# One search in lockstep on two engines, a buffer of its own for the pooling input, and two key blocks in one bank, in a hybrid attention layer

## The chip, the cores and the metric

One Trainium2 chip, one of its cores. The metric is the device time of one execution in microseconds (us), the median of several runs; lower is better. Engines are named as in the profile: PE (matrix multiply; PEld its weight loads), DVE (vector), ACT (scalar, activations), POOL (GpSimd), SP (issues the DMAs).

## What is computed

A layer of 1024 tokens and 1024 channels in float32. One input projection of the normalized tokens feeds three mixers, whose gated outputs are concatenated, projected and added to the input:

```python
h = rmsnorm(x, norm_g[layer])
z = jnp.einsum('bld,dc->blc', h, w_in[layer])
(pv, pg, dq, dk, dv, dg, iq, ik, iw, fq, fk, fv, fg, ff) = split_columns(z)
a_out = pool_mixer(pv, pool_w[layer], pool_scale[layer]) * jax.nn.silu(pg)
...
b_out = b_o.reshape(B, L, DSA_WIDTH) * jax.nn.silu(dg)
...
c_out = c_o.reshape(B, L, FOX_WIDTH) * jax.nn.silu(fg)
mixed = jnp.concatenate([a_out, b_out, c_out], axis=-1)
x = x + jnp.einsum('blc,cd->bld', mixed, w_out[layer])
```

The pooling mixer takes trailing-window means (windows 2, 4, 8, 16). The sparse mixer has an indexer (8 heads of 32 channels) that scores each key for each query as a weighted sum of relu'd dots; a query attends, in 6 heads, to its 256 best keys. The forgetting mixer is causal attention in 6 heads with a cumulative bias.

## The kernel before

Tokens are tiled by 128 (tiles 0 to 7). Every product of float32 data is split: a value is rounded to a high part (ACT copies it), the rest is a low part (DVE or POOL subtracts), and a projection sums three matmuls, high by high, high by low and low by high (`mm3`, L457). A chunk of a projection is 24 such matmuls of 384 or 512 columns into one PSUM bank of three (`pj`); then ACT and DVE evacuate it: L718 and L719 (queries and keys), L732 and L734 (gates), L659 and L660 (values), L1042 (pooling input, on ACT alone). The next matmul into that bank waits for the evacuation. Weights are split on ACT (L689, L433) and POOL (L690, L434).

The indexer's scores of tiles 2 to 7 (tile i has 128(i+1) keys) are summed on DVE (L602) and POOL closes each with a small fill (L605). Then `search` finds, for each query, the 256th best score by bisection over the 31 bits of a float: a round counts the scores above a trial value in each tile, compares the counts with 256 and sets the next bit. One search counts tiles 6 and 7 on ACT (L768, a sign with an accumulated sum, read out by a second instruction), another counts tiles 2 to 5 on DVE (L772). Each has its own three small DVE steps a round: L786, L788 and L789; L788 needs the counts of all tiles of its search, and the next round's counts need L789. There are 32 counts of each tile. `finish` turns the thresholds into masks (L813 to L843), with a correction (`fix`) for tiles counted on ACT.

The pooling mixer works in two halves, m = 0 and 1. A half has an input buffer `v`, filled by two L1042 on ACT, and two work buffers; POOL adds shifted copies (L1049), DVE takes the means (L1065 to L1069) and PE maps them (L1073). The three buffers of one half come from one tag, `pq`, that has three slots, so the second half's `v` gets a slot when the first half is through with it.

Attention goes in units of two heads by 512 queries: scores (L918, L921), maximum (L929), exponentials (L940), then for each block of 128 keys transpositions on PE (L950), their split by ACT (L957) and DVE (L959), and the products with the values (L963, L965). The last two key blocks of a head have only 256 and 128 columns. A unit ends with L975 to L998; at the end the output projection (`outproj`) runs on all engines.

Nothing of the order is written by hand. `Plan.schedule` is a list scheduler: from estimated durations (`t_mm`, `t_act`, `t_dve`, `t_pool`), priorities and free buffer slots it fixes one order for each engine before the run, and each engine runs its own in that order. A changed estimate, tag or list of tiles so moves instructions all over the kernel.

## Time and profile before

| what | value |
|---|---|
| median of 3 runs | 678.64 us (677.1 to 679.01) |
| the profiled execution | 675.91 us |
| its span | 674.1 us |
| PE busy | 631.3 us, 94% of the span |
| DVE busy | 524.4 us, 78% |
| ACT busy | 395.9 us, 59% |
| POOL busy | 202.5 us, 30% |

The span runs from the first to the last instruction of the program; the execution's own time is 1.8 us longer. The page shows the busy time of each engine, the same in 40 slices of the span with the clock granted to PE, and the costliest groups of instructions. The trace behind it answers questions on one engine, line or stretch: a timeline (instructions in order, equal neighbours merged, in brackets the idle time before and what ended it), waits, groups by line, and sums over a stretch. L457 is line 457 of the kernel before.

### The profile page before, as it was taken

To read this page: it belongs to the slowest core of one execution; us is meant where nothing else is said; L and a number is where in the kernel's file an instruction comes from. 1 tells how busy PE (TensorE), PEld (TensorE's weight loads), DVE (VectorE), ACT (ScalarE), POOL (GpSimd) and SP (SyncE) were. 2 spreads that over 40 slices of the span, in tenths; PEclk is the share of its full clock that TensorE was granted. 3 is DMA by queue.
4 is the path that set the end of the run, shared out by engine and by line. 5 is a ranking of instruction groups with operands and counts; after the bars stand their busy time and mean duration, and the time that the engine had idled before them with its cause. 6 is when DMAs were issued, how large, how long until landed. Compare 5 with 4: busy or idle time off the path is not lost. (4 is left out here: it accounts for less than half of the span.)

```text
span 674.1 us, 10707 instructions
## 1 busy us (share of the span) xinstructions
PE 631.3 (94%) x3278; PEld 529.4 (79%) x3278; DVE 524.4 (78%) x1363; ACT 395.9 (59%) x904; POOL 202.5 (30%) x218
## 2 busy tenths in 40 slices
PE   7899999999999399879999899999899999989995
PEld 5798777799888399667878688888778777778884
DVE  5978999999999989989997666758576868655322
ACT  5745777566666545531658467778567869731211
POOL 3610324520036512114442442512031435132311
PEclk9999999999999699989999999999899999999999
DMA  7707554640035323744647668569874555266211
GB/s 227 222 1 199 152 167 110 184 132 3 16 97 138 84 104 106 220 144 135 209 156 236 188 171 236 180 189 276 227 233 151 184 175 172 64 196 202 103 63 62
DMA packets 98439, 103.02 MB, mean 153 GB/s; under 512 B 10983, under 2 KB 67399, under 8 KB 98382
## 3 DMA queue, kind: packets, MB, share of 16 engines
q1 hardware_dynamic: 98382, 102.34, 50.8%
q8 instruction: 26, 0.43, 0.3%
q14 instruction: 31, 0.25, 0.1%
HBM read 72.35 MB, written 29.96 MB: 152 GB/s over the span
## 5 line engine op out<-in xcount | busy, mean ns | idle before, releaser
L457 PE MATMUL bank<-RA 128*128 128x512 f32 (+2 forms) x2016 | 492.0, 381 | 16.5 <-ACT FA L1042 10.5
L457 PEld LDWEIGHTS bank<-RA 128*128 128x128 f32 x2016 | 361.2, 190 | 67.6 <-ACT FA L1042 10.9
L957 ACT ACTIVATE RA<-bank 128x512 fp32r<-128x512 f32 (+3 forms) x144 | 67.8, 488 | 62.9 <-PE bank L950 58.8
L772 DVE TENSOR_SCALAR_CACHE_REDUCE FA<-FA 128x384 bf16<-128x384 f32 (+3 forms) x128 | 103.4, 808 | 1.6
L690 POOL TENSOR_TENSOR RA<-FA,RA 128x512 fp32r<-128x512 f32 x44 | 63.8, 1461 | 126.8 <-ACT RA L689 122.0
L768 ACT ACTIVATE FA<-FA 128x896 bf16<-128x896 f32 x64 | 69.8, 1090 | 52.6 <-DVE FA L789 42.9
L929 DVE CUSTOM_DVE_ANT_0 FA<-bank,FA 128x512 f32<-128x512 f32 (+3 forms) x144 | 77.4, 552 | 28.5 <-PE bank L921 9.9
L959 DVE TENSOR_TENSOR RA<-bank,RA 128x512 fp32r<-128x512 f32 (+3 forms) x144 | 77.0, 553 | 23.1 <-ACT RA L957 14.0
L940 ACT ACTIVATE FA<-FA 128x512 f32<-128x512 f32 (+3 forms) x144 | 86.8, 607 | 7.3 <-DVE FA L935 7.2
L950 PE MATMUL bank<-FA 128*128 128x128 f32 x432 | 79.4, 276 | 3.2 <-DVE RA L959 2.2
L950 PEld LDWEIGHTS bank<-FA 128*128 128x128 f32 x432 | 55.7, 141 | 21.3 <-DVE RA L959 5.3
L918 PE MATMUL bank<-RA 128*128 128x512 f32 (+3 forms) x144 | 52.3, 365 | 6.0 <-DVE FA L929 2.9
L602 DVE SCALAR_TENSOR_TENSOR FA<-FA 128x512 f32<-128x512 f32 (+3 forms) x70 | 54.2, 798 | 1.9
L921 PE MATMUL bank<-RA 128*128 128x512 f32 (+3 forms) x144 | 51.1, 361 | 2.6 <-DMA RA<-qk_dq 2.4
L965 PE MATMUL bank<-RA 128*128 128x512 f32 (+3 forms) x144 | 53.4, 375 | 0.0
L963 PE MATMUL bank<-RA 128*128 128x512 f32 (+3 forms) x144 | 49.2, 342 | 0.5 <-ACT RA L957 0.5
L594 ACT ACTIVATE FA<-bank 128x512 f32<-128x512 f32 (+3 forms) x80 | 39.7, 527 | 16.3 <-DVE FA L602 6.8
L925 POOL TENSOR_TENSOR FA<-FA 128x128 f32<-128x128 f32 x48 | 25.6, 541 | 71.2 <-DMA FA<-nf_d 34.9
L918 PEld LDWEIGHTS bank<-RA 128*128 128x128 f32 x144 | 27.1, 189 | 13.3 <-DVE FA L929 7.7
L921 PEld LDWEIGHTS bank<-RA 128*128 128x128 f32 x144 | 27.3, 191 | 6.2 <-DMA RA<-qk_dq 2.6
L963 PEld LDWEIGHTS bank<-RA 128*128 128x128 f32 x144 | 27.3, 190 | 6.3 <-ACT RA L957 2.1
L997 POOL TENSOR_TENSOR FA<-FA 128x512 f32<-128x512 f32 x12 | 16.2, 1347 | 52.9 <-DVE FA L993 27.6
(145 smaller groups left out, 688.1 us busy)
## 6 DMA issues: line engine op xcount, KB each, us to landing
FA<-in_w_in_dram SPq DMA_DIRECT2D x60, 256.0 KB, 3.4
FA<-in_x_dram SPq DMA_DIRECT2D x15, 512.0 KB, 3.6
RA<-qk_fq SPq DMA_DIRECT2D x48, 128.0 KB, 3.9
RA<-qk_dq SPq DMA_DIRECT2D x48, 128.0 KB, 2.8
RA<-qk_dk SPq DMA_DIRECT2D x36, 128.0 KB, 3.3
FA<-in_w_out_dram SPq DMA_DIRECT2D x16, 256.0 KB, 2.8
out_dram<-FA SPq DMA_DIRECT2D x7, 512.0 KB
RA<-qi SPq DMA_DIRECT2D x24, 128.0 KB, 3.0
```

The costliest lines, as they stand in the source:

```text
L457: M(lambda: nc.tensor.matmul(p()[:, :n], fa(), fb(), start=st, stop=sp), n, keys, [p], pr)
L690: G(lambda raw=raw, s=s: nc.gpsimd.tensor_tensor(Wl()[:, s, :], raw(), f32(Wh()[:, s, :]), op=OP.subtract), 512, [raw, (Wh, kh)], [(Wl, kh ...
L768: A(lambda c=c, i=i, jk=jk, s=s: nc.scalar.activation(jk(), SC[i](), AF.Sign, bias=s(), scale=-1.0, accum_out=cn()[:, c:c + 1]), n, sck(i) ...
L772: V(lambda c=c, i=i, jk=jk, s=s: nc.vector.tensor_scalar(jk(), SC[i](), s(), None, op0=OP.is_lt, op1=OP.add, accum_out=cn()[:, c:c + 1]), ...
L918: M(lambda s=s, k=k, n=n, j=j, hd=hd: nc.tensor.matmul(s()[:, :n], qx()[:, hd, j * 128:j * 128 + 128], k()[:, hd, :n], start=True, stop=Fa ...
L921: M(lambda s=s, k=k, n=n, j=j, hd=hd: nc.tensor.matmul(s()[:, :n], ql()[:, hd, j * 128:j * 128 + 128], k()[:, hd, :n], start=False, stop=T ...
L929: V(lambda s=s, Pt=Pt, n=n, u=u, j=j, mx=mx, bias=bias: nc.vector.tensor_tensor_reduce(Pt()[:, :n], s()[:, :n], bias()[:, u * 512:u * 512 ...
L940: A(lambda Pt=Ps[j][u], n=n, j=j, u=u, hd=hd, nm=nm: nc.scalar.activation(Pt()[:, :n], Pt()[:, :n], AF.Exp, bias=nm()[:, j:j + 1], accum_o ...
L950: M(lambda pt=pt, j=j, Pt=Ps[j][kb // 4], c=kb % 4 * 128: nc.tensor.transpose(pt()[:, j * 128:j * 128 + 128], Pt()[:, c:c + 128], ident()) ...
L957: A(lambda ph=ph, pt=pt, c=c: nc.scalar.activation(ph()[:, c], pt()[:, c], AF.Copy), n, [pt], [ph], pr, psum=True)
L959: V(lambda ph=ph, pl=pl, pt=pt, c=c: nc.vector.tensor_tensor(pl()[:, c], pt()[:, c], f32(ph()[:, c]), op=OP.subtract), n, [pt, ph], [pl], pr)
L963: M(lambda o=o, v=v, ph=ph, c=c, kb=kb: nc.tensor.matmul(o()[:, c], v(), ph()[:, c], start=(kb == 0), stop=False), n, kv + [ph], [o], pr)
```

## The change

1. `search` is called once, for all six tiles: tiles 5, 6 and 7 are counted on ACT, tiles 2, 3 and 4 on DVE, in lockstep: one L788 needs the counts of all six. `finish` goes over all tiles in order and corrects tiles 5, 6 and 7.
2. The pooling's `v` has a tag of its own, `pv`, with two slots, one of them new memory; `pq` keeps two slots for the work buffers.
3. The last two key blocks of a head are transposed into one bank and split by one ACT and one DVE instruction of 384 columns.
4. The scheduler takes a transposition for 0.07 us instead of 0.107, and adds 0.085 us to a PE instruction that follows one and is none itself.

```diff
-                    t = free[e]
+                    t = free[e] + (0.085 if e == PE and was_tr and not o.tr else 0.0)
...
+            if e == PE:
+                was_tr = o.tr
...
-    return max(n * 0.41667e-3 + 0.003, 0.107)
+    return 0.07 if n < 0 else max(n * 0.41667e-3 + 0.003, 0.107)
...
-    lay("F", f1 + 9 * KB, [("pq", 4160, 3), ("pw", KB, 1)], 1)
+    lay("F", f1 + 9 * KB + 4160, [("pq", 4160, 2), ("pw", KB, 1)], 1)
...
-    FSZ, RSZ = max(f2, f3), r3
+    FSZ, RSZ = max(f2, f3) + 4160, r3
+    P.tag("pv", "F", 4160, [FSZ - 4160, f1 + 9 * KB], 1)
...
-    M = lambda fn, n, r, w, pr=0.0: P.op(PE, fn, t_mm(n), r, w, pr)
+    M = lambda fn, n, r, w, pr=0.0: P.op(PE, fn, t_mm(n), r, w, pr, tr=n < 0)
...
-    def search(tiles, a):
-        nq = len(tiles)
-        eng = ACT if a == "a" else DVE
+    def search(tiles, on_act):
+        nq, a = len(tiles), "s"
         t0, _ = carve(nq)
         t1, _ = carve(nq)
         cn, _ = carve(nq)
@@ -754,21 +758,22 @@
         k = lambda nm, c=None: (cc, "s" + a, nm, c)
         for c, i in enumerate(tiles):
             n = (i + 1) * 128
-            G(lambda c=c, n=n: nc.gpsimd.memset(th()[:, c:c + 1],
-                                                float(n - 2 * TOPK if eng == ACT else n - TOPK) + 0.5), 1, [],
+            G(lambda c=c, i=i, n=n: nc.gpsimd.memset(th()[:, c:c + 1],
+                                                     float(n - (2 * TOPK if i in on_act else TOPK)) + 0.5), 1, [],
               [k("th")], 0)
         pr = PR_SEL
 
         def count(t, kt):
-            for c, i in enumerate(tiles):
+            for c, i in sorted(enumerate(tiles), key=lambda x: x[1] not in on_act):
                 n = (i + 1) * 128
                 s = (lambda: 0.0) if t is None else (lambda c=c: t()[:, c:c + 1])
-                jk = P.new("jka" if eng == ACT else "jkv", [128, n], BF)
-                if eng == ACT:
+                if i in on_act:
+                    jk = P.new("jka", [128, n], BF)
                     A(lambda c=c, i=i, jk=jk, s=s: nc.scalar.activation(jk(), SC[i](), AF.Sign, bias=s(), scale=-1.0,
                                                                          accum_out=cn()[:, c:c + 1]), n,
                       sck(i) + kt, [jk, k("cn", c)], pr, acc=True)
...
-    def finish(tiles, t, kt, cn, a, fix):
+    def finish(tiles, on_act, t, kt, cn, a):
         pr = PR_SEL
         v = nc.vector
-        if fix:
-            nz, knz = carve(len(tiles))
-            V(lambda: v.tensor_scalar(nz().bitcast(I32), t().bitcast(I32), 0x7fffffff, None, op0=OP.bitwise_and), 2,
-              [kt], [knz], pr)
-            V(lambda: v.tensor_scalar(nz(), nz(), 2.0 ** -126, None, op0=OP.is_ge), 2, [knz], [knz], pr)
-            V(lambda: v.tensor_tensor(t(), t(), nz(), op=OP.mult), 2, [kt, knz], [kt], pr)
-        for c, i in enumerate(tiles):
+        na = len(on_act)
+        nz, knz = carve(na)
+        ta = lambda: t()[:, :na]
+        V(lambda: v.tensor_scalar(nz().bitcast(I32), ta().bitcast(I32), 0x7fffffff, None, op0=OP.bitwise_and), na,
+          [kt], [knz], pr)
+        V(lambda: v.tensor_scalar(nz(), nz(), 2.0 ** -126, None, op0=OP.is_ge), na, [knz], [knz], pr)
+        V(lambda: v.tensor_tensor(ta(), ta(), nz(), op=OP.mult), na, [kt, knz], [kt], pr)
+        for c, i in sorted(enumerate(tiles), key=lambda x: x[1]):
+            fix = i in on_act
...
-            for kb in range(nkb):
-                j0 = max(0, kb - 4 * g)
+            v = lambda kb, h=h: VV[kb]()[:, h * 128:h * 128 + 128]
+            for kbs in [(kb,) for kb in range(nkb - 2)] + [(nkb - 2, nkb - 1)]:
                 pt = P.new("pt", [128, 512])
-                for j in range(j0, 4):
-                    M(lambda pt=pt, j=j, Pt=Ps[j][kb // 4], c=kb % 4 * 128: nc.tensor.transpose(
-                        pt()[:, j * 128:j * 128 + 128], Pt()[:, c:c + 128], ident()), 128,
-                      [Ps[j][kb // 4], k_ident], [pt], pr)
+                cols = []
+                for kb in kbs:
+                    j0 = max(0, kb - 4 * g)
+                    d = 256 if kb == nkb - 1 else 0
+                    cols.append((kb, j0, slice(j0 * 128 - d, 512 - d)))
+                    for j in range(j0, 4):
+                        M(lambda pt=pt, j=j, d=d, Pt=Ps[j][kb // 4], c=kb % 4 * 128: nc.tensor.transpose(
+                            pt()[:, j * 128 - d:j * 128 - d + 128], Pt()[:, c:c + 128], ident()), -128,
+                          [Ps[j][kb // 4], k_ident], [pt], pr)
                 ph = P.new("ph", [128, 512], F32R)
                 pl = P.new("pl", [128, 512], F32R)
-                c = slice(j0 * 128, 512)
-                n = 512 - j0 * 128
+                c = slice(min(x.start for _, _, x in cols), 512)
+                n = 512 - c.start
                 A(lambda ph=ph, pt=pt, c=c: nc.scalar.activation(ph()[:, c], pt()[:, c], AF.Copy), n, [pt], [ph],
                   pr, psum=True)
                 V(lambda ph=ph, pl=pl, pt=pt, c=c: nc.vector.tensor_tensor(pl()[:, c], pt()[:, c], f32(ph()[:, c]),
                                                                            op=OP.subtract), n, [pt, ph], [pl], pr)
-                v = lambda kb=kb, h=h: VV[kb]()[:, h * 128:h * 128 + 128]
-                kv = [(VV[kb], "h"), (VV[kb], "l")]
-                M(lambda o=o, v=v, ph=ph, c=c, kb=kb: nc.tensor.matmul(o()[:, c], v(), ph()[:, c], start=(kb == 0),
-                                                                       stop=False), n, kv + [ph], [o], pr)
-                M(lambda o=o, v=v, pl=pl, c=c, kb=kb, nkb=nkb: nc.tensor.matmul(
-                    o()[:, c], v(), pl()[:, c], start=False, stop=(kb == nkb - 1)), n, kv + [pl], [o], pr)
+                for kb, j0, c in cols:
+                    kv = [(VV[kb], "h"), (VV[kb], "l")]
+                    M(lambda o=o, v=v, ph=ph, c=c, j0=j0, kb=kb: nc.tensor.matmul(
+                        o()[:, j0 * 128:], v(kb), ph()[:, c], start=(kb == 0), stop=False), 512 - j0 * 128, kv + [ph], [o],
+                      pr)
+                for kb, j0, c in cols:
+                    kv = [(VV[kb], "h"), (VV[kb], "l")]
+                    M(lambda o=o, v=v, pl=pl, c=c, j0=j0, kb=kb, nkb=nkb: nc.tensor.matmul(
+                        o()[:, j0 * 128:], v(kb), pl()[:, c], start=False, stop=(kb == nkb - 1)), 512 - j0 * 128,
+                      kv + [pl], [o], pr)
...
-        v, s1, s2 = (P.new("pq", [128, W]) for _ in range(3))
+        v, s1, s2 = P.new("pv", [128, W]), P.new("pq", [128, W]), P.new("pq", [128, W])
...
-    sa = search([6, 7], "a")
-    sv = search([2, 3, 4, 5], "v")
-    finish([2, 3, 4, 5], *sv, False)
-    finish([6, 7], *sa, True)
+    on_act = [5, 6, 7]
+    tiles = on_act + [2, 3, 4]
+    finish(tiles, on_act, *search(tiles, on_act))
```

In the other places (`op`, `norm`, `idx_k`, `idx_tile`, `forget`, `unit`) a transposition only gets the width -128, by which the scheduler knows it.

What this does to the order of the instructions is shown at three places. In the rows of the changed kernel line numbers are its own: L768 became L772, L772 became L777, L786, L788 and L789 became L791, L793 and L794, L689 L694, L732 L737, L659 and L660 L664 and L665, and L1042 L1058.

ACT at the pooling, before; the counts of the search are L768, the weight splits L689:

```order
L768 ACTIVATE FA<-FA 128x896
L768 ACTIVATE FA<-FA 128x1024
L689 ACTIVATE RA<-FA 128x512 x2
L1042 ACTIVATE FA<-bank_66 128x512
L1042 ACTIVATE FA<-bank_65 128x512
L659 ACTIVATE RA<-bank_71 128x3x2x64
```

The same place now:

```order
L1058 ACTIVATE FA<-bank_71 128x512
L772 ACTIVATE FA<-FA 128x1024
L772 ACTIVATE FA<-FA 128x768
L772 ACTIVATE FA<-FA 128x896
L772 ACTIVATE FA<-FA 128x1024
L1058 ACTIVATE FA<-bank_65 128x512
L694 ACTIVATE RA<-FA 128x512 x2
L772 ACTIVATE FA<-FA 128x768
L772 ACTIVATE FA<-FA 128x896
L664 ACTIVATE RA<-bank_66 128x3x2x64
```

The second half's two evacuations stood together, after the splits; now they stand a round and a third apart, each as its chunk comes.

DVE in one round of the search, in the stretch of the sparse values, before (128x2 belongs to the search on ACT, 128x4 to the one on DVE):

```order
L786 TENSOR_SCALAR FA<-FA 128x2
L772 TENSOR_SCALAR FA<-FA 128x384
L786 TENSOR_SCALAR FA<-FA 128x4
L772 TENSOR_SCALAR FA<-FA 128x512
L772 TENSOR_SCALAR FA<-FA 128x640
L660 TENSOR_TENSOR RA<-bank_66,RA 128x3x128
L788 TENSOR_TENSOR FA<-FA 128x2
L772 TENSOR_SCALAR FA<-FA 128x768
L789 SCALAR_TENSOR_TENSOR FA<-FA 128x2
L788 TENSOR_TENSOR FA<-FA 128x4
L786 TENSOR_SCALAR FA<-FA 128x2
L789 SCALAR_TENSOR_TENSOR FA<-FA 128x4
```

A round there now:

```order
L777 TENSOR_SCALAR FA<-FA 128x384
L791 TENSOR_SCALAR FA<-FA 128x6
L777 TENSOR_SCALAR FA<-FA 128x512
L777 TENSOR_SCALAR FA<-FA 128x640
L665 TENSOR_TENSOR RA<-bank_71,RA 128x3x128
L793 TENSOR_TENSOR FA<-FA 128x6
L794 SCALAR_TENSOR_TENSOR FA<-FA 128x6
```

The count of 768 is gone from DVE, and one trio of small steps is left, with the evacuation of a value chunk just ahead of it.

ACT at the end of the search, before, up to the first gate of the forgetting mixer:

```order
L768 ACTIVATE FA<-FA 128x1024
L689 ACTIVATE RA<-FA 128x512 x2
L768 ACTIVATE FA<-FA 128x896
L768 ACTIVATE FA<-FA 128x1024
L768 ACTIVATE FA<-FA 128x896
L732 ACTIVATE FA<-bank_65 128x512
```

And now:

```order
L772 ACTIVATE FA<-FA 128x1024
L694 ACTIVATE RA<-FA 128x512 x2
L772 ACTIVATE FA<-FA 128x768
L772 ACTIVATE FA<-FA 128x896
L772 ACTIVATE FA<-FA 128x1024
L772 ACTIVATE FA<-FA 128x768
L772 ACTIVATE FA<-FA 128x896
L772 ACTIVATE FA<-FA 128x1024
L737 ACTIVATE FA<-bank_65 128x512
```

The first gate stood before the last count; now it stands behind the last round, the fifth after the last value chunk.

## Rows read from the trace of the kernel before

**Rows 1.** Page, part 1: busy us (share of the span) x instructions of each engine.

```profile
PE 631.3 (94%) x3278; PEld 529.4 (79%) x3278; DVE 524.4 (78%) x1363; ACT 395.9 (59%) x904; POOL 202.5 (30%) x218
```

**Rows 2.** Timeline of PE, 195 to 305 us; in brackets the idle time before and its releaser.

```profile
194.79 27.47 PE L457 MATMUL bank<-RA 128*128 128x512 f32 x126
232.81 15.71 PE L457 MATMUL bank<-RA 128*128 128x384 f32 x75 [10.55 <-ACT FA L1042]
...
292.24 12.98 PE L457 MATMUL bank<-RA 128*128 128x512 f32 x49 [3.75 <-DVE FA L734]
```

**Rows 3.** PE's waits, whole span: us in total, times, longest us.

```profile
PE bank L918 <- DVE FA L929: 2.9, 3, 2.2
PE bank L921 <- DMA RA<-qk_dq: 2.4, 1, 2.4
...
PE bank L918 <- DMA RA<-qk_fq: 2.0, 1, 2.0
```

**Rows 4.** Three stretches: busy us by engine, granted clock (PEclk), DMA share, GB/s.

```profile
75.00:136.00 61.00, 59.17 (x257) 46.17 (x258) 59.67 (x100) 42.23 (x88) 20.66 (x18) 1.00 0.54 149
224.50:238.00 13.50, 5.19 (x16) 5.19 (x17) 13.36 (x45) 8.28 (x15) 5.41 (x6) 0.50 0.25 73
292.80:296.00 3.20, 3.20 (x9) 2.44 (x8) 3.20 (x8) 1.14 (x2) 0.00 (x0) 0.50 0.42 164
```

**Rows 5.** Timeline of ACT: first count of tile 7, the late evacuation, the first gate.

```profile
136.05 1.06 ACT L768 ACTIVATE FA<-FA 128x1024 bf16<-128x1024 f32 x1 [3.54 <-POOL FA L605]
...
232.16 1.09 ACT L1042 ACTIVATE FA<-bank 128x512 f32<-128x512 f32 x2 [3.29 <-DVE FA L789]
...
290.86 0.60 ACT L732 ACTIVATE FA<-bank 128x512 f32<-128x512 f32 x1 [3.17 <-DMA mx_p<-FA]
```

**Rows 6.** DVE by line: counts, then compare and step: busy us, mean ns.

```profile
L772 DVE TENSOR_SCALAR_CACHE_REDUCE FA<-FA 128x384 bf16<-128x384 f32 (+3 forms) x128 | 103.4, 808 | 1.6
...
L788 DVE TENSOR_TENSOR FA<-FA 128x4 int32<-128x4 f32 (+1 forms) x62 | 16.3, 278 | 1.0 <-ACT FA L768 1.0
L789 DVE SCALAR_TENSOR_TENSOR FA<-FA 128x4 int32<-128x4 int32 (+1 forms) x62 | 15.1, 260 | 0.1
```

**Rows 7.** Timeline of ACT in one round: tile 6, its readout, tile 7, its readout.

```profile
202.18 1.04 ACT L768 ACTIVATE FA<-FA 128x896 bf16<-128x896 f32 x1 [0.29 <-DVE FA L789]
203.13 0.19 ACT L768 ACTIVATION_READ_ACCUMULATOR FA<-FA 128x1 f32 x1
203.35 1.15 ACT L768 ACTIVATE FA<-FA 128x1024 bf16<-128x1024 f32 x1
204.41 0.19 ACT L768 ACTIVATION_READ_ACCUMULATOR FA<-FA 128x1 f32 x1
```

**Rows 8.** Timeline of all engines at 242.38 us: DVE's step, then ACT's next count.

```profile
242.38 0.16 DVE L789 SCALAR_TENSOR_TENSOR FA<-FA 128x2 int32<-128x2 int32 x1
...
242.63 1.04 ACT L768 ACTIVATE FA<-FA 128x896 bf16<-128x896 f32 x1 [1.29 <-DVE FA L789]
```

**Rows 9.** ACT by line and shape: value evacuation and weight split.

```profile
L659 ACT ACTIVATE RA<-bank 128x384 fp32r<-128x384 f32 x16 | 7.6, 477 | 4.8 <-PE bank L457 4.7
...
L689 ACT ACTIVATE RA<-FA 128x512 fp32r<-128x512 f32 x44 | 27.1, 630 | 7.1 <-DMA FA<-nf_d 1.9 <-DMA FA<-in_w_in_dram 1.9 <-PE bank L457 1.8
```

**Rows 10.** Timeline of PE in attention: a lone transposition, and three in a run.

```profile
394.78 0.27 PE L950 MATMUL bank<-FA 128*128 128x128 f32 x1
...
402.24 0.49 PE L950 MATMUL bank<-FA 128*128 128x128 f32 x3
402.48 0.48 PE L965 MATMUL bank<-RA 128*128 128x512 f32 x1
402.80 0.39 PE L963 MATMUL bank<-RA 128*128 128x512 f32 x1
```

**Rows 11.** ACT by line and shape: the last two evacuations of a head.

```profile
L957 ACT ACTIVATE RA<-bank 128x256 fp32r<-128x256 f32 x24 | 9.1, 380 | 17.5 <-PE bank L950 17.4
...
L957 ACT ACTIVATE RA<-bank 128x128 fp32r<-128x128 f32 x24 | 6.6, 273 | 5.5 <-PE bank L950 5.5
```

More of the change, by code (lines that the diff above doesn't have):

```diff
@@ L77 @@
 class Op:
-    __slots__ = ("eng", "fn", "dur", "pr", "seq", "deps", "bufs", "outs", "end", "left", "bytes", "lag")
+    __slots__ = ("eng", "fn", "dur", "pr", "seq", "deps", "bufs", "outs", "end", "left", "bytes", "lag", "tr")
 class Plan:
@@ L516, in norm @@
                 c = (4 * u + k) * 128
-                M(lambda p=p, k=k, c=c: nc.tensor.transpose(p()[:, k, :], xt()[:, c:c + 128], ident()), 128,
+                M(lambda p=p, k=k, c=c: nc.tensor.transpose(p()[:, k, :], xt()[:, c:c + 128], ident()), -128,
                   [(xt, u), k_ident], [p], pr)
@@ L557, in idx_k @@
         pk = P.new("s", [128, 512])
[L558 removed]
+        M(lambda: nc.tensor.transpose(pk()[:, :128], zt()[:, 0, :], ident()), -128, [zt, k_ident], [pk], pr)
         kk = lambda: KI()[:, i * 128:i * 128 + 128]
@@ L569, in idx_tile @@
         for u in range(2):
-            M(lambda u=u: nc.tensor.transpose(pq()[:, u, :], Z[i]()[:, u * 128:u * 128 + 128], ident()), 128,
+            M(lambda u=u: nc.tensor.transpose(pq()[:, u, :], Z[i]()[:, u * 128:u * 128 + 128], ident()), -128,
               [Z[i], k_ident], [pq], pr)
@@ L771, in count @@
                 else:
+                    jk = P.new("jkv", [128, n], BF)
                     V(lambda c=c, i=i, jk=jk, s=s: nc.vector.tensor_scalar(jk(), SC[i](), s(), None, op0=OP.is_lt,
@@ L974, in unit @@
         pr8 = P.new("pt", [128, 512])
-        M(lambda: nc.tensor.transpose(pr8()[:8, :128], rc().rearrange("p h j -> p (h j)"), ident()), 128,
+        M(lambda: nc.tensor.transpose(pr8()[:8, :128], rc().rearrange("p h j -> p (h j)"), ident()), -128,
           [rc, k_ident], [pr8], pr)
```

7 lines of the change are left out of this document (4 added, 3 removed).

## The prediction, made before the changed kernel ran

> **What bounds the kernel now.** I read the page first: PE is busy 94% of the span [rows 1], so a gain is either less work on PE or less waiting by PE. The counts of PE's instructions do not change, so it must be waiting. The timeline of PE shows where: the two longest waits of the run, 10.55 us for L1042 (pooling input) and 3.75 us for L734 (a gate) [rows 2], and 2.0 us for a query load close to them [rows 3]. The sums over stretches show what waiting costs on top: after the first wait PE's granted clock is 0.50 (1.2 of 2.4 GHz) and PE works 5.19 us in that stretch, half of it lost, 2.6 us; after the second it works 3.20 us at 0.50, 1.6 us lost [rows 4]. Together 10.55 + 3.75 + 2.0 + 2.6 + 1.6 = 20.5 us.
>
> Both long waits come from the search. The timeline of ACT [rows 5] shows L1042 starting at 232.16, after 3.29 us of idle ACT: its buffer was held by the pooling's first half, whose DVE steps stood in DVE's queue between the counts. The first gate of the forgetting mixer starts at 290.86, behind the last rounds of the search. So from 136.05, when tile 7 is first counted, to 290.86 the two searches pace the program through the queues of ACT and DVE, and PE has three banks to run ahead with. The question for the change is when its single search ends.
>
> **Term 1, the search starts earlier.** From 75 to 136 us DVE is busy 59.67 of 61 us [rows 4]: the sums of tile 7 are late because of DVE's queue. Before the last of them stood ten counts and six small steps; by the order now stand three counts and no step. Seven counts at 0.808 and six steps at about 0.27 [rows 6] are 5.7 + 1.6 = 7.3 us. PE's last dots also stand earlier in its order. Tile 7's first count: 136.05 - 7.3 = 128.8. (Bounds: 136.05 if nothing of it arrives.)
>
> **Term 2, a round.** ACT now has the longest part. Tile 6 takes 1.17 us to the next start, tile 7 1.25 us to the end of its readout; 128 columns are worth 1.15 - 1.04 = 0.11, so tile 5 takes 1.06 [rows 7]. Together 3.48. DVE's three counts, at most 3 x 0.808 = 2.4, lie beside it. Then comes the handoff that nothing hides: L788 and L789 at 0.16 each, and a passing on of 0.09 (ACT starts at 242.63, the step ended at 242.54) at either end [rows 8]: 0.50. A round is 3.98, and 31 rounds after the first 123.4 us.
>
> Some steps take far longer than 0.16: the means are 0.278 and 0.260 [rows 6], so the excess is (0.118 + 0.100) x 62 = 13.5 us over two searches. One search has half of these steps: 6.8 us (bounds 0 and 13.5). The Trainium skill ("SBUF — State Buffer", Who interferes with whom) has a DVE instruction with two inputs in SBUF and a GpSimd instruction that reads SBUF lock each other out for a whole instruction; it speaks against a lockstep, in which ACT's tiles now wait too. By that rule the excess lies where POOL is busy, and the sum stays as it is.
>
> **Term 3, what else is in ACT's queue.** By the order 16 value evacuations at 0.48 [rows 9], 11 others at 0.60 [rows 5] and 24 splits at 0.63 [rows 9]: 7.7 + 6.6 + 15.1 = 29.4. Neighbours overlap by 0.1 (two L1042 in 1.09 [rows 5]): 51 x 0.1 off, 24.3. In 12 rounds one of them stands ahead of the first count and fills the handoff, 12 x 0.45 = 5.4 off: 18.9. Splits wait for their loads now and then: 7.1 us of idle before 44 of them [rows 9], of which I take 2 us for these 24 (bounds 0 and 7).
>
> **The sum for the search.** 128.8 + 1.25 (tile 7 of the first count) + 123.4 + 6.8 + 18.9 + 2 = 281.1. From the first gate on ACT to the matmul that waits for it go 292.24 - 290.86 = 1.4 us [rows 2, 5], so PE goes on at 282.5 instead of 292.24: 9.7 us earlier. The old gate also waited 3.17 us for a pooling store [rows 5]. In the new order the last store's DVE step stands at the head of the last round, some 3.5 us before the gate, so I take nothing for it; if the store is late behind SP's loads, up to 3 us come back.
>
> **What PE does meanwhile.** The new `v` slot removes the wait of 10.55 us; its work is hidden in nothing, the wait simply has no cause left. But PE does not win it: without all its losses it would want the fourth gate bank at 292.24 - 10.55 - 3.75 - 2.0 - 2.6 = 273.3, and finds it at 282.5. So a new wait of some 9 us is late next, at L734's successor, and by the stretch after the 10.55 us wait it costs 2.6 us of clock where the old wait there cost 1.6: 1.0 us back. The tile 5 correction adds a count of 768 and six small steps to `finish` on DVE, beside PE's gate chunks; nothing for it.
>
> **Transpositions together.** PE's order has 53 runs of transpositions less (227 to 174). A run of three takes 402.24 to 402.48 and lengthens the next matmul to 0.32, against 27.47/126 = 0.22 for one in a stream [rows 2, 10]: 0.34, or 0.11 each. In the durations, two more add 0.49 - 0.27 = 0.22 [rows 10], again 0.11 each, so a change-over is worth about 0.01 and not the scheduler's 0.085: 53 x 0.01 = 0.5 us (bounds 0 and 4.5).
>
> **The shared bank.** It saves 24 ACT instructions: the two now take 0.380 + 0.273 [rows 11]; by the difference for 128 columns, 0.107, one of 384 takes 0.49, so 0.16 x 24 = 3.9 us of ACT, and as much of DVE. Both lie beside PE's matmuls; only ends of heads can feel it. I take 0.5 us (bounds -2 and 4: the last block's transpositions now all precede its split).
>
> **Total.** 9.7 - 1.0 + 0.5 + 0.5 = 9.7 us. The profiled execution took 675.9 us, so 666.2; it is 2.7 us under the median of 678.64, and against that the forecast is 668.9 us.
>
> **Rivals.**
> Slower: DVE, not ACT, ends the rounds. In DVE's new order the subtraction of an evacuated chunk stands just ahead of the step. If it ends the round, each of 27 rounds pays it, at least as long as ACT's half, 0.48 to 0.60 [rows 5, 9]: 27 x 0.55 = 14.9 us, 683.8 us. It decides from 9.7/31 = 0.31 us a round. For it: DVE's steps do stretch. Against: DVE's counts need 2.4 us of 3.48, and ACT mostly evacuates ahead of tile 7's 1.25 us.
>
> PE stops waiting: the search ends 9 us earlier than I think, which needs no excess and handoffs nearly filled. Then all 20.5 us go: 678.64 - 20.5 - 1 = 657.1 us. Against it: 3.48 us of counts alone leave little to save.
>
> Attention gives it back. After 300 us PE waits for L929 and for loads, 2.9 and 2.4 us [rows 3], little; but its order is new everywhere. Two new waits like the 3.75 with their drop (5.35 each) give 679.6, no change. For it: nothing but the priorities looks after these waits. Against: plenty of projection matmuls are left to fill with.
>
> Grouping cools PE. In this trace the clock fell only after PE had idled [rows 2, 4]. The Trainium skill ("TensorE: Matmul & The Clock Gate", Part 4: PE-mode transpose) says that transpositions do not count as PE being busy, which speaks against longer runs. Three drops like the 1.6 us one would make 673.7 us.
>
> **How the numbers follow.** A measurement of this kernel can tell about 0.3%, 2 us, from no change. Forecast 0.58 (its own range 662 to 677, by the bounds of terms 1 to 3), DVE ends the rounds 0.15, PE stops waiting 0.08, attention 0.15, cooling 0.04. Faster gets 0.56 of the forecast, PE's 0.08, a third of attention and most of cooling: 0.72. No change takes the forecast's upper edge and half of attention: 0.12. Slower takes the first rival and the rest of attention's: 0.16. The range, 657 to 682, reaches to the full gain below and almost to the first rival above.
>
> **What would show it.** Right: no wait for the pooling evacuation; tile 7's first count near 129; rounds of 4.0 to 4.9 us on ACT with no long idle; the first gate near 281 on ACT; PE's longest wait, 7 to 11 us, just before it, with one drop of the clock; PE's busy time within 2 us. Wrong: ACT idle for DVE's step more than 0.8 us a round, a first gate later than 290, a clock below 1.00 in attention without a wait, or new waits of over 5 us after 310.

## The result, and the profile after

The changed kernel takes 662.04 us (median of 4 runs, 660.23 to 663.12) against 678.24 us before (677.1 to 679.01): a ratio of 0.9769, with a 95% interval of 0.974 to 0.9799. It is faster, as forecast, by 16.2 us in the place of 9.7, and inside the range of 657 to 682. The profiled execution took 663.12 us with a span of 661.4; the one before took 675.91 with 674.1, so between the two profiles lie 12.7 us of span. Further lines have moved: L457 is now L462, L734 is L739, L950 is L962, L1049 is L1065, L1053 is L1069, L1065 is L1081, L1073 is L1089.

The first part of the page, which answers to [rows 1]:

```profile
span 661.4 us, 10577 instructions
...
PE 626.0 (95%) x3278; PEld 528.8 (80%) x3278; DVE 473.6 (72%) x1187; ACT 425.5 (64%) x944; POOL 197.8 (30%) x218
```

DVE has 50.8 us of work less, ACT 29.6 more, and PE 5.3 less, with the same 3278 matmuls. The timeline of PE from 255 to 310 us, for [rows 2]:

```profile
269.92 0.34 PE L928 MATMUL bank<-RA 128*128 128x384 f32 x1
276.27 25.36 PE L462 MATMUL bank<-RA 128*128 128x512 f32 x99 [6.01 <-DVE FA L739]
```

The wait of 10.55 us for L1042 and the 2.0 us for a query load are gone. One wait of 6.01 us for the first gate is left, and it ends at 276.27 us, 16.0 us earlier than the 3.75 us one did. Windows (columns as in [rows 4]) show the one drop of the clock behind it, to 1.2 of 2.4 GHz, and its end:

```profile
275.00:281.90 6.90, 5.63 (x13) 4.46 (x14) 6.33 (x17) 2.16 (x4) 0.00 (x0) 0.51 0.20 77
281.90:300.00 18.10, 18.10 (x81) 14.94 (x80) 16.61 (x29) 3.63 (x7) 6.33 (x5) 1.00 0.40 104
```

ACT's timeline, for [rows 5] and [rows 7]: the first count of tile 7, one undisturbed round (the next starts at 259.45), the last readout, and the first gate with the wait ahead of it:

```profile
124.67 1.06 ACT L772 ACTIVATE FA<-FA 128x1024 bf16<-128x1024 f32 x1 [1.78 <-POOL FA L610]
...
255.48 0.94 ACT L772 ACTIVATE FA<-FA 128x768 bf16<-128x768 f32 x1 [0.50 <-DVE FA L794]
...
256.55 1.04 ACT L772 ACTIVATE FA<-FA 128x896 bf16<-128x896 f32 x1
...
257.71 1.15 ACT L772 ACTIVATE FA<-FA 128x1024 bf16<-128x1024 f32 x1
...
259.45 0.94 ACT L772 ACTIVATE FA<-FA 128x768 bf16<-128x768 f32 x1 [0.49 <-DVE FA L794]
...
271.11 0.19 ACT L772 ACTIVATION_READ_ACCUMULATOR FA<-FA 128x1 f32 x1
274.90 1.30 ACT L737 ACTIVATE FA<-bank 128x512 f32<-128x512 f32 x2 [3.61 <-DMA mx_p<-FA]
```

The last row matters most: the search is over at 271.3 us, and the gate still waits 3.61 us for a store of the pooling, mx_p. (`mx_p` is the pooled output. Its store reads one of the two buffers `th`, which the gate's first step, on ACT, writes next.) The pooling's last two DVE steps end at 267.1 and 269.1 us; SP's queue shows their stores behind loads of queries, keys and weights, issued from 270.65 on:

```profile
260.81 6.01 SPq L365 DMA_DIRECT2D RA<-qk_fq  x8
266.86 2.51 SPq L365 DMA_DIRECT2D RA<-qk_fk  x4
269.48 1.08 SPq L365 DMA_DIRECT2D FA<-in_w_in_dram  x2
270.65 0.93 SPq L365 DMA_DIRECT2D mx_p<-FA  x2
```

**Where the time went.** For each profiled run I add up what PE loses: its idle time, and half of the time that it works at a granted clock of 0.50. The rest, to PE's last instruction, is its own work.

| us | before | after | difference |
|---|---|---|---|
| lost, 0 to 130 us | 8.4 | 9.1 | +0.7 |
| lost, 130 to 300 us | 20.9 | 8.9 | -12.0 |
| lost, after 300 us | 11.9 | 12.7 | +0.8 |
| PE's own work | 625.4 | 623.2 | -2.2 |
| end of PE's work | 666.7 | 653.9 | -12.7 |

(The sums were made before rounding.) So the time came out of the stretch of the search. What in the change brought it there is the question for the experiments.

### The profile page after: what moved, and what is told of

Same layout as the page of the kernel before. It is cut to its first block, busy times and chain, and to the rows that moved or that the text cites. A ratio compares the mean times of both kernels' runs of the same rounds, so it can differ in the third digit from the quotient of the medians.

```text
span 661.4 us, 10577 instructions
## 1 busy us (share of the span) xinstructions
PE 626.0 (95%) x3278; PEld 528.8 (80%) x3278; DVE 473.6 (72%) x1187; ACT 425.5 (64%) x944; POOL 197.8 (30%) x218
## 5 line engine op out<-in xcount | busy, mean ns | idle before, releaser
L462 PE MATMUL bank<-RA 128*128 128x512 f32 (+2 forms) x2016 | 484.5, 378 | 8.9 <-DVE FA L739 6.0
L462 PEld LDWEIGHTS bank<-RA 128*128 128x128 f32 x2016 | 360.7, 189 | 60.4 <-DVE FA L739 6.3
L772 ACT ACTIVATE FA<-FA 128x768 bf16<-128x768 f32 (+2 forms) x96 | 99.4, 1036 | 18.4 <-DVE FA L794 15.4
L969 ACT ACTIVATE RA<-bank 128x512 fp32r<-128x512 f32 (+1 forms) x120 | 63.8, 553 | 53.5 <-PE bank L962 51.5
L971 DVE TENSOR_TENSOR RA<-bank,RA 128x512 fp32r<-128x512 f32 (+1 forms) x120 | 73.4, 632 | 23.6 <-ACT RA L969 22.8
L777 DVE TENSOR_SCALAR_CACHE_REDUCE FA<-FA 128x384 bf16<-128x384 f32 (+2 forms) x96 | 71.2, 742 | 1.9
L962 PE MATMUL bank<-FA 128*128 128x128 f32 x432 | 71.8, 273 | 0.1
L962 PEld LDWEIGHTS bank<-FA 128*128 128x128 f32 x432 | 54.4, 140 | 18.1 <-DVE RA L971 2.4
L925 PE MATMUL bank<-RA 128*128 128x512 f32 (+3 forms) x144 | 52.9, 368 | 3.5 <-DVE FA L936 3.5
L928 PE MATMUL bank<-RA 128*128 128x512 f32 (+3 forms) x144 | 51.0, 356 | 4.1 <-DMA RA<-qk_dq 4.0
L607 DVE SCALAR_TENSOR_TENSOR FA<-FA 128x512 f32<-128x512 f32 (+3 forms) x70 | 52.1, 762 | 2.4
L975 PE MATMUL bank<-RA 128*128 128x512 f32 (+3 forms) x144 | 45.8, 345 | 3.5 <-ACT RA L969 3.5
L980 PE MATMUL bank<-RA 128*128 128x512 f32 (+3 forms) x144 | 48.0, 361 | 0.0
L975 PEld LDWEIGHTS bank<-RA 128*128 128x128 f32 x144 | 26.7, 189 | 9.9 <-ACT RA L969 6.2
L925 PEld LDWEIGHTS bank<-RA 128*128 128x128 f32 x144 | 27.2, 189 | 9.0 <-DVE FA L936 5.1
L1146 DVE TENSOR_TENSOR FA<-bank,FA 128x512 f32<-128x512 f32 x16 | 11.0, 688 | 31.4 <-PE bank L462 31.4
(145 smaller groups left out, 678.5 us busy)
```

The lines of the kernel that those rows point to most:

```text
L462: M(lambda: nc.tensor.matmul(p()[:, :n], fa(), fb(), start=st, stop=sp), n, keys, [p], pr)
L607: V(lambda rl=rl, w=w, acc=acc, wc=wc: nc.vector.scalar_tensor_tensor(acc(), rl()[:, :w], wc(), acc(), op0=OP.mult, op1=OP.add), w, [rl, ( ...
L772: A(lambda c=c, i=i, jk=jk, s=s: nc.scalar.activation(jk(), SC[i](), AF.Sign, bias=s(), scale=-1.0, accum_out=cn()[:, c:c + 1]), n, sck(i) ...
L777: V(lambda c=c, i=i, jk=jk, s=s: nc.vector.tensor_scalar(jk(), SC[i](), s(), None, op0=OP.is_lt, op1=OP.add, accum_out=cn()[:, c:c + 1]), ...
L925: M(lambda s=s, k=k, n=n, j=j, hd=hd: nc.tensor.matmul(s()[:, :n], qx()[:, hd, j * 128:j * 128 + 128], k()[:, hd, :n], start=True, stop=Fa ...
L962: M(lambda pt=pt, j=j, d=d, Pt=Ps[j][kb // 4], c=kb % 4 * 128: nc.tensor.transpose(pt()[:, j * 128 - d:j * 128 - d + 128], Pt()[:, c:c + 1 ...
```

## The experiments

Twelve kernels ran, in three sets, each beside the kernel before on its chip. The first theory was the prediction's: the search's end sets when PE goes on, and the gain is an earlier end. The table has the same sums for all of them.

| kernel | median us | ratio to before (95%) | lost 130 to 300 | lost after 300 | PE's own work |
|---|---|---|---|---|---|
| before, own v buffers (e1) | 674.9 | 0.9968 (0.9939 to 0.9996) | 19.1 | 10.2 | 623.6 |
| before, lockstep alone (e2) | 665.7 | 0.9842 (0.9816 to 0.9867) | 5.3 | 16.2 | 621.9 |
| after, two searches (e3) | 665.27 | 0.9831 (0.9806 to 0.9856) | 15.5 | 8.8 | 619.8 |
| after, own slots for the pooling's gates (e4) | 660.19 | 0.975 (0.9717 to 0.9782) | 3.6 | 12.2 | 622.6 |
| before, transpositions priced (e5) | 673.69 | 0.9935 (0.9906 to 0.9964) | 18.7 | 11.6 | 621.2 |
| before, shared bank (e6) | 674.39 | 0.9965 (0.9948 to 0.9982) | 21.9 | 11.0 | 624.5 |
| before, other tie-break (e7) | 678.02 | 1.0009 (0.9982 to 1.0035) | 21.8 | 15.1 | 623.0 |
| after, other tie-break (e8) | 664.32 | 0.9806 (0.9776 to 0.9836) | 7.9 | 15.1 | 621.9 |
| before, pooling held back 3 us, not 12 (e9) | 666.74 | 0.9835 (0.98 to 0.987) | 13.0 | 11.3 | 623.7 |
| after, the same (e10) | 666.7 | 0.983 (0.9792 to 0.9867) | 2.6 | 21.0 | 622.7 |
| before, priced in the front alone (e11) | 672.05 | 0.9906 (0.9873 to 0.9939) | 21.3 | 11.5 | 619.7 |
| after, own slots and 3 us (e12) | 653.98 | 0.964 (0.9604 to 0.9676) | 3.1 | 13.1 | 622.0 |

The sums belong to one profiled execution, the medians to 4 to 12. "Before" ran at 676.9 to 678.5 us in the three sets. Between 0 and 130 us, which the table leaves out, PE loses 7.0 to 13.1 us; the eight profiled executions with 10.0 or more (e1, e2, e3, e5, e7, e8, e9, e10) have drops of the clock before 31 us, which none of the other six has.

### e1: own buffers for v, alone

```diff
-    lay("F", f1 + 9 * KB, [("pq", 4160, 3), ("pw", KB, 1)], 1)
+    lay("F", f1 + 9 * KB + 4160, [("pq", 4160, 2), ("pw", KB, 1)], 1)
...
+    P.tag("pv", "F", 4160, [FSZ - 4160, f1 + 9 * KB], 1)
...
```

> The kernel before with one part added, the pooling buffers of their own for v. Theory (the end of the search paces TensorE; the time is gained because the search ends earlier): the 10.55 us wait for the pooling evacuation goes, but the search still ends near 290 us, so TensorE waits for the first gate of the forgetting mixer instead, some 10 to 14 us in the place of 3.75; the run stays within 3 us of the 678 us of the kernel before (675 to 681). Rival A (the wait of 10.55 us and its 2.6 us of clock were themselves the loss, and the own buffers are the gain): 665 us, with a first gate that is no longer waited for by more than 4 us.

Measured: 0.3%, some 2 us. PE's timeline (the three longest of its six waits between 225 and 300 us) shows why:

```profile
229.45 6.03 PE L458 MATMUL bank<-RA 128*128 128x384 f32 x24 [1.96 <-ACT FA L1043]
...
272.41 0.76 PE L919 MATMUL bank<-RA 128*128 128x512 f32 x1 [4.59 <-DMA RA<-qk_fq]
291.78 8.60 PE L458 MATMUL bank<-RA 128*128 128x512 f32 x30 [3.24 <-DVE FA L735]
```

The wait of 10.55 us is 1.96, but PE goes on behind the gate at 291.8 us as before, and on the way there it idles elsewhere: of 16.6 us without work between 130 and 300 us 13.0 are left. The 10 to 14 us of waiting were expected at the gate itself; there it is 3.24 us, and the rest lies ahead of it. Rival A falls: a wait that is taken away ahead of a later gate is mostly paid again before that gate.

### e2 and e3: the lockstep alone, and everything but the lockstep

```diff
-    sa = search([6, 7], "a")
-    sv = search([2, 3, 4, 5], "v")
+    on_act = [5, 6, 7]
+    tiles = on_act + [2, 3, 4]
+    finish(tiles, on_act, *search(tiles, on_act))
```

e2 puts this, with the new `search` and `finish`, into the kernel before; e3 takes it out of the changed one.

> The kernel before with one part added, the single lockstep search with tile 5 on ACT. Theory: the search starts near 125 us and its last count ends near 271 to 275 us, so nearly the whole of the 16 us comes from this part: 661 to 668 us, with a wait of TensorE for the pooling's evacuation that may be left, but lies before an earlier end of the search. Rival A (own buffers are the gain): 674 us or more, with the 10 us wait for the pooling evacuation as before. Rival B (the list order as a whole, or transpositions together and the shared bank, are the gain): 672 us or more.

> The changed kernel with one part undone: two searches again, tile 5 on VectorE; own buffers for v, shared bank and the priced transpositions stay. Theory: tile 7's first count goes back to about 136 us, the last count to about 290, and the time to 674 to 680 us, with one long wait of TensorE for the first gate. Rivals A and B (own buffers, or the grouping and the bank, carry the gain): 660 to 668 us.

e2 gave 1.6%, about 10.7 us, as expected, though its last count starts at 282.0 us and not before 275. **e3 missed**: without the lockstep 11.4 us of the gain are still there. The two sum to 22 us where all parts together gave 16: they overlap. And both traces speak against the first theory. ACT's timeline in e2, gates between the search's last counts:

```profile
274.82 0.60 ACT L732 ACTIVATE FA<-bank 128x512 f32<-128x512 f32 x1 [3.77 <-DMA mx_p<-FA]
275.31 1.03 ACT L767 ACTIVATE FA<-FA 128x896 bf16<-128x896 f32 x1
...
282.04 1.14 ACT L767 ACTIVATE FA<-FA 128x1024 bf16<-128x1024 f32 x1
```

and in e3, where the last count of tile 7 ends at 278.1 and the gate is 7.6 us later:

```profile
276.94 1.15 ACT L773 ACTIVATE FA<-FA 128x1024 bf16<-128x1024 f32 x1
...
285.75 1.23 ACT L737 ACTIVATE FA<-bank 128x512 f32<-128x512 f32 x2 [7.56 <-DMA mx_p<-FA]
```

In one run the gate goes 7 us before the last count, in the other 9 us after it. What it waits for in both is mx_p, the store that ends the pooling. The lockstep's part in this: the pooling's DVE steps stand in DVE's queue behind counts. Before, the first step stood behind four counts and two searches' small steps (here from the first of those counts); DVE's timeline:

```profile
225.49 0.61 DVE L772 TENSOR_SCALAR_CACHE_REDUCE FA<-FA 128x384 bf16<-128x384 f32 x1
...
227.86 1.01 DVE L772 TENSOR_SCALAR_CACHE_REDUCE FA<-FA 128x768 bf16<-128x768 f32 x1
...
228.79 1.98 DVE L1065 SCALAR_TENSOR_TENSOR FA<-FA 128x1024 f32<-128x1024 f32 x1
```

With the lockstep alone that step starts at 219.5 us, in the changed kernel at 218.8, and the second half's at 250.7 and 249.6 where it was 265.8. Only a part of that is DVE's queue. The step needs the last of POOL's sums for its half, the copy at L1053, which ends at 221.2 us before, at 215.4 with the lockstep alone and at 212.7 in the changed kernel. So DVE's queue holds the first half's step for 7.6, 4.1 and 6.0 us, and the second half's for 7.9, 5.2 and 6.1.

### e4: the pooling's gates get slots of their own

The pooling loads its gates back into the two buffers (`th`) that the forgetting mixer's gates need.

```diff
+    P.tag("pth", "F", 2 * KB, [f1 + 2 * KB * q for q in range(4)], 1)
...
-            gt = P.new("th", [128, 512])
+            gt = P.new("pth", [128, 512])
```

> The changed kernel with four buffers of their own for the gates that the pooling loads back (they stood in the two buffers of the tanh outputs, which the forgetting mixer's gates need). In the order the first three gates of the forgetting mixer now stand on ACT between the last rounds of the search. Theory: TensorE's wait of 6.0 us before the first gate and the stretch at clock 0.50 behind it (about 1.7 us lost) are due to those buffers and not to the end of the search as such; without them TensorE has projections to go on with until the search is over: 654 to 657 us, and no wait of over 4 us between 260 and 300 us. Rival C (TensorE waits for the end of the search whatever the buffers are, since the attention behind it needs the masks): 660 to 664 us, with the wait moved to the chunks after the gates.

The wait and the drop of the clock went. ACT's timeline has the gates among the rounds, none of them waiting for mx_p:

```profile
257.32 0.57 ACT L738 ACTIVATE FA<-bank 128x512 f32<-128x512 f32 x1
...
273.93 1.15 ACT L773 ACTIVATE FA<-FA 128x1024 bf16<-128x1024 f32 x1
```

The search ends 4 us later here than in the changed kernel, and PE loses 5.3 us less between 130 and 300. So PE does not wait for the search's end as such, and the wait did not move on to later chunks, as rival C has it. By the time alone this run tells nothing: 654 to 657 us were expected, the profiled run took 655.5, but the median of six is 660.2, inside rival C's 660 to 664, and there is no profile of a slower run to say what those lost. The mean granted clocks on record do not settle it: 0.992 in the profiled run, but 661.7 us at 0.990 and 658.4 at 0.987. e9 and e12 had to settle the cause.

### e5 to e8: the price of transpositions, the bank, and the order as a lottery

e5 has the price (its two main lines are below) in the kernel before, e6 the shared bank, e7 and e8 change a tie-break and nothing else.

```diff
-                    t = free[e]
+                    t = free[e] + (0.085 if e == PE and was_tr and not o.tr else 0.0)
...
-    return max(n * 0.41667e-3 + 0.003, 0.107)
+    return 0.07 if n < 0 else max(n * 0.41667e-3 + 0.003, 0.107)
```

```diff
-                lim = tmin + .003
+                lim = tmin + .006
```

> The kernel before with one part added: the planner's price for a change-over from a transposition to a matmul (0.085 us) and its shorter duration for a transposition (0.07). The run with two searches and all other parts was 1.7% faster than before, which the end of the search can't explain (it went on at 287.1 us against 292.2). Theory now: the end of the search is one of two sources of equal size, and the other lies in the list order that these prices make; a run with them alone then takes 667 to 672 us. Rival A (own buffers are needed for it): 675 us or more. Rival D (any other order gives as much, a lottery of the list): the run with no part changed and another tie-break moves as far as this one.

> The kernel before with one part added, the bank that the last two key blocks share; transpositions are priced as before. Theory: 24 instructions of 0.16 us fewer on ACT and on VectorE, beside matmuls: 0.5 us, bounds +2 and -4, so 673 to 679 us. Rival: the bank is the other source of the gain, 666 to 671 us.

> The kernel before with nothing changed but the planner's tie-break: operations that could start within 0.006 us of the earliest count as equal, in the place of 0.003. It makes another order of much the same plan. Theory: within 3 us of before, 674 to 680 us. Rival D (the order is a lottery whose prizes are as large as what is to be explained): 6 us or more to either side.

> The changed kernel with nothing changed but the same tie-break, 0.006 in the place of 0.003 us. Theory: within 3 us of the changed kernel, a ratio to before of 0.972 to 0.982. Rival D: 5 us or more to either side, a ratio under 0.970 or over 0.984.

The price alone gave 4.4 us, the bank 2.4, the own buffers (e1) 2.2: each clear of no change, e1 barely (its interval ends at 0.9996), 9.0 together, and 11.4 measured as one (e3). The tie-break moved the kernel before by 0.6 us, which is no change, and the changed one by some 2.5 us, in two intervals that overlap; in both profiles more is lost after 300 us (15.1, against 11.9 and 12.7). Rival D, in its strong form, falls; but a rebuilt order alone may be worth some 2 us, which is the size of e1 and e6 alone.

What the price does is not what the prediction looked at. PE's timeline in e5, in the front of the kernel, then ACT's:

```profile
33.86 0.27 PE L574 MATMUL bank<-FA 128*128 128x128 f32 x1
33.97 0.60 PE L521 MATMUL bank<-FA 128*128 128x128 f32 x4
```

```profile
125.01 1.06 ACT L772 ACTIVATE FA<-FA 128x1024 bf16<-128x1024 f32 x1 [1.54 <-POOL FA L609]
...
277.08 1.15 ACT L772 ACTIVATE FA<-FA 128x1024 bf16<-128x1024 f32 x1
278.13 0.18 ACT L772 ACTIVATION_READ_ACCUMULATOR FA<-FA 128x1 f32 x1
285.94 0.60 ACT L736 ACTIVATE FA<-bank 128x512 f32<-128x512 f32 x1 [7.62 <-DMA mx_p<-FA]
```

L574 transposes the index queries of tile 2. Beside a run of other transpositions they now stand at 34 us; before, ACT evacuated them at 50.5 us. With them the dots and the search come earlier: tile 7 is first counted at 125.0 in the place of 136.05 us, and its last count starts at 277.1, not 291.4. Yet the gate goes only 4.9 us earlier, again behind mx_p.

### e9, e10 and e12: the pooling chain itself

If mx_p is the pacer, the chain that ends in it must have become as much shorter as the gate came earlier. Its steps, from the traces (us):

| step | before | after |
|---|---|---|
| POOL's last sum of the first half ends | 221.15 | 212.74 |
| its DVE step starts | 228.79 | 218.77 |
| the last small DVE step of that half ends | 232.30 | 222.51 |
| its projection starts on PE | 248.36 | 234.03 |
| POOL's last sum of the second half ends | 257.85 | 243.56 |
| its DVE step starts | 265.76 | 249.63 |
| the last small DVE step of that half ends | 267.82 | 251.32 |
| its projection starts on PE | 281.23 | 264.09 |
| the first gate starts on ACT | 290.86 | 274.90 |

The halves are tied together: POOL's sums of the second wait for the projection of the first, which reads a work buffer that they need. POOL's timeline before (L1053 is the copy that ends a half's sums):

```profile
220.10 1.05 POOL L1053 COPY FA<-FA 64x1024 f32<-64x1024 f32 x1
...
250.39 6.37 POOL L1049 TENSOR_TENSOR FA<-FA 128x1024 f32<-128x1024 f32 x3 [15.07 <-PE bank L1073]
```

and after:

```profile
211.71 1.03 POOL L1069 COPY FA<-FA 64x1024 f32<-64x1024 f32 x1
```

Of the 16.0 us by which the gate came earlier, 8.4 were there at the chain's start (ACT takes up the half's input 5.3 us earlier, at 199.16 for 204.50), 3.5 are less waiting in DVE's queue, and 4.5 are the place of the first projection in PE's order; the rest cancels but for 0.4 us.

One number sets that place. The planner holds the pooling's projection on PE back by 12 us, once in each half: in the kernel before it stood 16.1 and 13.4 us behind the half's last DVE step, in the changed one 11.5 and 12.8 (in e1 and e3 9.0 and 7.1 in the first half, so the "13 to 16 us" expected of all traces, below, holds for some of them). With 3 us in e9 it is 5.9 and 1.6.

```diff
-                                                         start=True, stop=True), 0.858, kp + [pw], [py], pr, lag=12.0)
+                                                         start=True, stop=True), 0.858, kp + [pw], [py], pr, lag=3.0)
```

> The kernel before with one number changed: the 12 us by which the planner holds back the pooling's projection matmul behind its DVE step are 3 us. In all traces so far the pooling's projection stands 13 to 16 us behind its step, in each of the two halves, and the first gate of the forgetting mixer follows the store behind the second. Theory now (a chain through the pooling paces that gate, not the last round of the search): the gates start before the last rounds of the search, at 270 us or earlier, TensorE's wait there (3.75 us and 1.6 us of clock) goes, and the run takes 669 to 674 us; the wait of 10.55 us stays. First theory (the end of the search paces TensorE): 675 to 679 us, with the wait near 290 us in another place. Rival E (the 12 us cover a late DVE step): TensorE waits for the pooling's step, 5 us or more, and the run takes over 680 us.

> The changed kernel with the same number changed, 3 us in the place of 12. Theory: both halves of the pooling come 8 to 11 us earlier each, the gates start near 255 us, the 6.0 us wait at 276 and its 1.7 us of clock go: 654 to 660 us. First theory: 660 to 664 us, with TensorE waiting for the last rounds (270 us) at another place. Rival E: a wait for the pooling's step of over 4 us, 664 us or more.

> The changed kernel with both: own buffers for the gates that the pooling loads back, and 3 us in the place of 12. Theory: either of them takes the 6.0 us wait and its clock away, so the two together give no more than one, 653 to 660 us, within 2 us of the better of the two alone. Rival (the two add up, since each half of the pooling still holds something else): 650 us or less.

**e9 decides it.** PE's and ACT's timelines in e9, the kernel before with one number changed:

```profile
233.91 5.50 PE L457 MATMUL bank<-RA 128*128 128x384 f32 x19 [10.50 <-ACT FA L1042]
...
278.46 26.26 PE L457 MATMUL bank<-RA 128*128 128x512 f32 x115
```

```profile
275.46 0.58 ACT L732 ACTIVATE FA<-bank 128x512 f32<-128x512 f32 x1
275.94 1.14 ACT L768 ACTIVATE FA<-FA 128x1024 bf16<-128x1024 f32 x1
```

The wait for the pooling input is there in full and the last count of tile 7 starts at 288.5 us, 3 us earlier than in the kernel before; but the first gate goes at 275.5 (270 or earlier was expected), among the rounds, and PE never stops for it. That took 1.65% off, 11 us, more than the 4 to 9 expected and over four times what the tie-break moved. The profiled execution, the second slowest of six, shows 7.4 us of it at PE's end: 7.9 less lost between 130 and 300 us, 2.9 more in the front. Neither the first theory nor rival E has room for that.

In e10 the same edit removes the wait as well (lost 130 to 300: 2.6 us), yet the run takes 666.7 us, by the medians more than the changed kernel, where 654 to 660 were expected. This miss is a loss elsewhere. PE's waits (in total, times, longest) in attention and in the output projection are now these; the first was longer in the changed kernel (4.0 in two), the others are new:

```profile
PE bank L928 <- DMA RA<-qk_dq: 2.3, 1, 2.3
PE bank L925 <- DMA RA<-qk_dk: 2.2, 1, 2.2
...
PE bank L462 <- ACT RA L1133: 2.0, 1, 2.0
PE bank L975 <- DVE FA L1009: 2.0, 1, 2.0
PE bank L462 <- POOL RA L1134: 1.7, 1, 1.7
```

Three drops of the clock to 1.2 GHz stand behind such waits (all but the one for qk_dk): 21.0 us are lost after 300 us in the place of 12.7, and of the 8.3 us more 6.2 are the clock and 2.1 idle time. What makes those waits was not tried.

e12 has both edits and is the best of all, 653.98 us, 3.6% under the kernel before and, by intervals that do not touch, under the changed one. Its page:

```profile
span 652.6 us, 10578 instructions
...
PE 625.4 (96%) x3278; PEld 530.7 (81%) x3278; DVE 471.4 (72%) x1187; ACT 425.3 (65%) x944; POOL 203.3 (31%) x218
```

Two ways to remove one wait were expected to give no more than the better of them, within 2 us. The profiled spans do so, within 1.1 us of each other. The medians do not: e12 is 6.2 us under e4, by intervals that do not touch, while the rival's 650 us were not reached either. What e4's slower runs lost stays open, as said there.

### e11: the price in the front alone

The edit of e5 with `-128` at L517, L558 and L570 only.

> The kernel before with the planner's price for change-overs in its front alone (the transpositions of the normed rows, of the index keys and of the index queries); those of the attention and of the forget sums are priced as before. Theory: what the price gave (673.7 us with all of it) comes from the place of the index queries' transpositions: tile 2's stand at 35 us in the place of 50, the dots begin 7 us earlier, tile 7 is first counted near 125 us in the place of 136, and the pooling chain behind the counts in VectorE's queue ends earlier: 672 to 675 us. Rival F (the price pays in attention, where most of the transpositions are): 676 to 678 us, with tile 7's first count still near 125.

The front alone gave as much as the whole (6.4 us against 4.4, within the intervals), so rival F falls: the price does not pay in attention. But the way was another than expected. Tile 7 is first counted at 127.5 us, and still 21.3 us are lost between 130 and 300, as in the kernel before. The gain is in PE's own work, 5.7 us less. PE by line from 0 to 130 us (busy us, mean ns, idle), e11 first, then before:

```profile
L461 PE MATMUL bank<-RA 128*128 128x512 f32 (+1 forms) x451 | 101.6, 356 | 2.3 <-ACT RA L525 2.0 <-POOL RA L438 0.2
...
L521 PE MATMUL bank<-FA 128*128 128x128 f32 x64 | 9.5, 275 | 3.0 <-DVE FA L514 3.0
```

```profile
L457 PE MATMUL bank<-RA 128*128 128x512 f32 (+1 forms) x432 | 99.7, 358 | 2.2 <-ACT RA L521 1.6 <-POOL RA L434 0.4
...
L517 PE MATMUL bank<-FA 128*128 128x128 f32 x64 | 10.6, 287 | 2.4 <-DVE FA L510 1.3 <-DVE RA L522 0.8
```

Beside the same 80 dots and 92 transpositions PE gets 451 projection matmuls done in 130 us where it did 432: 19 more, at 0.23 us 4.4 us of work. By the time that each adds to the end of the one ahead, idle time taken off, a transposition of the normed rows costs 0.118 us against 0.135, and a dot of 512 columns 0.239 against 0.285.

## Why the prediction was right, and where it was not

The time is inside the range on the forecast's side, and the main place was right: the loss from 130 to 300 us. The step that failed is the one under the whole sum, "from 136.05 [...] to 290.86 the two searches pace the program". What paced PE there was the pooling's chain up to mx_p. In the ten traces with shared buffers and 12 us (before, after, e1 to e3, e5 to e8, e11) the first gate waits for mx_p; with buffers of its own (e4, e12) or 3 us (e9, e10) it does not, and in e9 it goes 13 us before the last count of tile 7. The search costs PE time where the pooling's steps stand behind its counts, and of the 16.0 us by which the gate moved DVE's queue is 3.5. That the search and the chain ended within 4 us of each other, before and after, is luck, and it is why a sum over rounds came near.

A premise ahead of it fell too: "The counts of PE's instructions do not change, so it must be waiting". With the same 3278 matmuls PE's own work is 2.2 us less in the changed kernel and 5.7 in e11.

- **Term 1** (tile 7 first counted at 128.8): 124.67, 11.4 us earlier and not 7.3. The cause was misread: lockstep alone gives 4.5 us (131.54 in e2), the price alone 11.0 (e5), and 8.5 with the price in the front alone (e11). And it is not worth its length: e11, which starts counting that much earlier, loses as much in the stretch as the kernel before.
- **Term 2**: right. A round takes 3.97 us (255.48 to 259.45), forecast 3.98. DVE's line summary gives the stretch of the small steps:

```profile
L793 DVE TENSOR_TENSOR FA<-FA 128x6 int32<-128x6 f32 x31 | 10.7, 344 | 25.4 <-ACT FA L772 25.4
...
L794 DVE SCALAR_TENSOR_TENSOR FA<-FA 128x6 int32<-128x6 int32 x31 | 6.2, 200 | 1.0
```

  Over 0.16 each that is (0.184 + 0.040) x 31 = 6.9 us, forecast 6.8. In e2 the same two take 218 and 167 ns on average, 2.0 us over in all; so the stretch is no constant of the lockstep. It lies where POOL is busy, as the prediction had it: 50 of the 62 steps overlap no POOL instruction and take at most 170 ns each, the other 12 take 713 on average.
- **Term 3**: the search took 146.6 us and not 152.3. Idle time on ACT in it is 18.8 us, just the 0.50 x 31 + 6.8 - 5.4 + 2 = 18.9 of the forecast; the other evacuations and splits took 21.4 us by the union of their spans and not 24.3, and the counts overlapped their neighbours as well, 106.3 us and not 109.1.
- **The store taken for nothing** ("if the store is late behind SP's loads, up to 3 us come back"): 3.61 us, and it was the pacer. 4.1 us from the start, 5.7 from the length and 3.6 back make the 6.2 us between 282.5 and 276.27.
- **What PE does meanwhile**: right in kind. One wait before the gate, 6.01 us for 9, one drop of the clock with 2.8 us lost for 2.6, no wait for the pooling input.
- **Transpositions together** (0.5 us): the price of a change-over was right, the term was not. In the trace after, a run of one, two, three or four transpositions in a stream adds about 0.117, 0.230, 0.338 and 0.452 us, within 0.02 of the trace before; but the planner's price moved the front, 4.4 us (e5) to 6.4 (e11).
- **The shared bank** (0.5 us): 2.4 us alone (1.2 to 3.5), not told apart from a new order.
- Of the signs **shown in advance**, ACT's idle time for the step is 0.50 us a round (15.4 us in 31; 1.8 in the longest, where 0.8 a round was the limit), rounds take 4.7 us on average (4.0 to 4.9), and no clock is below 1.00 in attention. Missed are the first count (124.67 for 129), the gate (274.90 for 281), the wait (6.01 for 7 to 11), and PE's busy time: 5.3 us less where 2 were allowed, 3.1 of them because PE worked less time at half clock and 2.2 its own work.
- The **rivals**: "DVE ends the rounds" did not come; "PE stops waiting", at 657.1 us, is what e12 reached, by another way. "Grouping cools PE" did not come: unbroken runs of up to 11 transpositions in the front stand at a granted clock of 1.00, and behind 281.9 us it stayed there to PE's last instruction. The Trainium skill ("TensorE: Matmul & The Clock Gate", Part 4: PE-mode transpose) says that transpositions do not count as PE being busy in the same way; nothing of that is visible at these lengths of run.
- The **chances** of "no change" and "slower" come to about 0.10 and 0.18 by the prediction's own parts, not 0.12 and 0.16.
